# Eight loads of key and value weights move from SyncE's queue to GpSimd's in a trunk layer's prologue

## The chip, the cores and the metric

The kernel runs on one core of a Trainium2 chip. A core has five engines with an instruction stream each: TensorE (PE) multiplies matrices, VectorE (DVE), ScalarE (ACT) and GpSimd (POOL) work on rows of 128 partitions, SyncE (SP) only issues transfers (DMAs). The engines meet at semaphores. Transfers issued by any engine are carried out by the core's 16 DMA engines. The metric is the time of one execution on the device in microseconds. Before the change it is 1074.85 us, the median of three runs (1074.67 to 1075.89).

## The reference

One layer of a diffusion backbone runs over 128 context tokens and 512 latent tokens, 640 rows of width 1024, in float32. The part that the change touches is the start: a modulation is worked out from two conditioning vectors, applied to the normalised tokens, and the keys and values are columns 1024 to 1535 of the product with `w_in`.

```python
ada_ctx = (jax.nn.silu(c_ctx) @ w_ada[i] + b_ada[i])[None, None, :]
ada_lat = (jax.nn.silu(c) @ w_ada[i] + b_ada[i])[:, None, :]
...
def trunk_layer(h, ada, p, rope_tabs, ctx_k, ctx_v):
    sh1, sc1, g1, sh2, sc2, g2 = jnp.split(ada, N_ADA, axis=-1)
    u = rms_norm(h, p["g_pre1"]) * (1 + sc1) + sh1
    mo, k, v = mixer(u, p, rope_tabs, ctx_k, ctx_v)
    h = h + g1 * rms_norm(mo, p["g_post1"])
    u = rms_norm(h, p["g_pre2"]) * (1 + sc2) + sh2
    h = h + g2 * rms_norm(conv_ffn(u, p), p["g_post2"])
    return h, k, v
...
def mixer(u, p, rope_tabs, ctx_k, ctx_v):
    z = u @ p["w_in"]
    ...
    q, k, v, b_gate, c_gate, x_in, g_att, g_conv = jnp.split(z, idx, axis=-1)
```

Behind it follow attention over latent and cached context keys, a gated convolution, the output projection, and a feed-forward part with a convolution of width 3.

## The kernel before

All products are made in three passes: each float32 operand is split into a rounded part (`whi`, `UH`) and the rest (`wlo`, `UL`), and PE multiplies high by high, high by low and low by high (`mm3`, lines 234 to 237).

The prologue computes the keys and values. Its steps are these.

- The tokens: five tiles of 128 rows, `XT[:, t, :]`, 0.52 MB each, are loaded by SP (line 410). For each tile ACT sums the squares (`square`, line 435), POOL makes the variance and its root (`rstd_of`, lines 282 and 283), DVE scales the rows (`normal`, line 440), PE turns them (`x_turn`, line 447), and ACT or DVE copies them out (`x_copy`, lines 453 and 455).
- The modulation: scale and shift of the 1024 features are worked out in six groups of one or two blocks of 128 features, `GROUPS = ((0,), (1,), (2, 3), (4, 5), (6,), (7,))`. A group of one block takes two loads of 0.52 MB of `w_ada`, a group of two takes four (`ada_loads`, line 405). They go to tiles called `araw` and, for later groups, into the room of token tiles that are used up. PE multiplies them with the conditioning vectors (`ada1_mm`, line 478), ACT copies the result (line 486), PE adds up the pieces (lines 491 to 498), and DVE writes scale and shift, `scsh` (lines 503 and 505).
- `modulate` (lines 520 to 524) makes block f of the modulated tokens, `UH` and `UL`, on ACT and DVE.
- The key and value weights come in eight units, one for each block of 128 features: 128x512 floats, 0.26 MB. `fetch(i)` loads all units below i that aren't loaded yet. There are three buffers called `raw`, of two units each: units 0 and 1 share the first (raw_161 in the lists below), 2 and 3 the second, 4 and 5 the third, 6 and 7 the first again. `cut_upto` splits a unit on ACT and DVE (lines 592 and 594 for the first, 200 and 201 for the others).
- PE adds up keys and values over the eight blocks for the five token tiles (`kv_first`, line 531, for part of block 0, then `kv_mm`, by lines 235 to 237).

Units 8 and 9 of `units` are later weights of 4x256 columns, and go through `fetch` too.

What sets the order: PE, ACT, DVE and, in the prologue, SP run their instructions in the order in which the code is written. POOL's are put in order by the scheduler of the framework, which may move an instruction ahead when its buffers are free. A load into a buffer that is in use waits on its queue until the readers are done, and so do all behind it.

Of the kernel before, what the change touches and what calls it, by code (L numbers as in the profile page):

```python
# [22 lines left out]
KT = 8  # L23
# [89 lines left out]
def trunk_layer(ctx, tc, x_prompt, x_sample, cache_k, cache_v, c, c_ctx, w_ada, b_ada, g_pre1, g_post1, g_pre2,  # L113
                g_post2, w_in, q_norm, k_norm, w_att_out, conv_w, w_conv_out, w_o, w_up, conv_ffn, w_down, rope,
                y_prompt, y_sample, new_k, new_v):
    nc = tc.nc
    V, S, G, PE = nc.vector, nc.scalar, nc.gpsimd, nc.tensor
# [52 lines left out]
    def ps1():  # L170
        turn[1] += 1
        return psa.tile([128, 512], F32, tag=f"s1{turn[1] % 2}", name=nm("s1"), bufs=1)
# [7 lines left out]
    state = {"next": 0, "raw": [], "cut": [], "limit": 10}  # L180

    def raw_tile():
        return wp.tile([128, 1024], F32, tag="raw", name=nm("raw"), bufs=3)
# [22 lines left out]
    def fetch(i):  # L206
        while len(state["raw"]) < min(i, len(units), state["limit"]):
            w, k0, nk, c0, n = units[len(state["raw"])]
            if nk * n > 512:
                raw = raw_tile()  # L210
            else:

                if not halves:
                    raw = raw_tile()
                    halves.extend([raw[:, 512:1024], raw[:, 0:512]])
                raw = halves.pop()
            nc.sync.dma_start(raw[:, :nk * n].rearrange("p (k c) -> p k c", c=n),
                              w[k0 * 128:(k0 + nk) * 128, c0:c0 + n].rearrange("(k p) c -> p k c", p=128))
            state["raw"].append(raw)

# [6 lines left out]
    def next_unit():  # L227
        i = state["next"]
        state["next"] += 1
        fetch(i + 3)  # L230
        cut_upto(i + 2)
        return state["cut"][i]
# [141 lines left out]
    with tc.tile_pool(name="pro", bufs=2) as pro, tc.manual_schedule(engines={mybir.EngineType.SP}):  # L374
# [34 lines left out]
        for t in range(NT):  # L409
            nc.sync.dma_start(XT[:, t, :], xrows(t))  # L410
        ada_loads(0, [araw_tile() for _ in range(2)])
        fetch(1)
        ada_loads(1, [araw_tile() for _ in range(2)])
        fetch(2)

        def features():
# [174 lines left out]
        raw = state["raw"][0][:, 0:512]  # L591
# [41 lines left out]
        for f in range(2, KT):  # L633
# [42 lines left out]
            if f == KT - 2:  # L676
                cut_upto(9)
                p = ps1()
# [568 lines left out]
    def bank(i):  # L1247
        if i >= 2 and len(pools) == 1:
            early.close()
            pools.append(ctx.enter_context(tc.tile_pool(name="pb", bufs=1, space=bass.MemoryType.PSUM)))  # L1250
        return pools[i >= 2].tile([128, 512], F32, tag=f"b{i}", name=nm(f"b{i}"))
# [784 lines left out]
    for q in range(4):  # L2036
# [11 lines left out]
        elif q == 1:  # L2048
            half_load(0)
            p = bank(6)  # L2050
# [18 lines left out]
        for t in range(NT):  # L2069
# [5 lines left out]
            if q == 3 and t == 2:  # L2075
                p = bank(7)
# [448 lines left out]
```

## Time and profile before

| | |
|---|---|
| median of three runs | 1074.85 us |
| profiled execution | 1074.79 us, of it a span of 1073.0 us from the first to the last instruction |
| busy in the span: PE, DVE, ACT, POOL | 98%, 84%, 56%, 12% |
| chain of waits: share of PE | 90% |
| mean granted PE clock | 0.999 of full speed |
| moved from and to memory | 164.02 MB, a mean of 153 GB/s |

The profile gives times from the first instruction on. "L217" is line 217 of the kernel; "SPq" is SP's instruction that issues a transfer, and its length is the time that the issue took, not that of the transfer. A bracket at the end of a row is the time that the engine stood idle ahead of it and who released it. PEld is PE's loading of weights, which runs beside PE's multiplication.

### The profile page before, as it was taken

The page shows a single profiled execution, that of the slowest core. Times are in us where ns is not written, and L with a number is a line of the kernel's source. Part 1 is how long each engine was busy: PE and PEld are TensorE (multiplying, and loading weights), DVE is VectorE, ACT ScalarE, POOL GpSimd, SP SyncE. Part 2 cuts the span into 40 slices and gives each one's busy share as a digit, 9 for nine tenths or more (in the row PEclk, how much of TensorE's full clock was granted, in tenths as well). Part 3 has the DMA queues.
Part 4 walks back from the last instruction along what each step waited for, and adds up shares of the span by engine and source line. Part 5 has one row for each costly group of instructions (what it writes and reads, how often), then busy time and mean ns, then how long its engine had stood idle before and what let it go on. Part 6 is the DMA issues. An engine that isn't in the chain of part 4 may idle for free.

```text
span 1073.0 us, 20652 instructions
## 1 busy us (share of the span) xinstructions
PE 1056.8 (98%) x8216; PEld 995.4 (93%) x8216; DVE 899.9 (84%) x1379; ACT 598.4 (56%) x1057; POOL 133.1 (12%) x162
## 2 busy tenths in 40 slices
PE   8999999999999999999999999999999999999997
PEld 6788898899999999999998789999999999999996
DVE  5699999865498999896599678889999988989897
ACT  5478999942344544445322366645555555546673
POOL 1087676500000000000000020000000000000001
PEclk9999999999999999999999999999999999999999
DMA  9829999962244333223668634434544534436873
GB/s 320 256 82 175 190 168 187 191 147 60 75 123 124 93 103 94 79 79 99 189 188 253 198 131 129 121 116 136 166 131 152 150 122 131 152 116 219 277 275 115
DMA packets 243197, 164.02 MB, mean 153 GB/s; under 512 B 94874, under 2 KB 216214, under 8 KB 243102
## 3 DMA queue, kind: packets, MB, share of 16 engines
q1 hardware_dynamic: 242990, 162.68, 55.5%
q8 instruction: 64, 1.05, 0.4%
q14 instruction: 31, 0.25, 0.1%
q10 hardware_dynamic: 112, 0.04, 0.0%
HBM read 123.31 MB, written 17.36 MB: 131 GB/s over the span
## 4 chain that ended last, share of the span: by engine, by line
PE 90%; DVE 3%; ACT 2%; DMA 1%; POOL 1%; issue 1%; SPq 1%; DVEq 0%; ACTq 0%; POOLq 0%
PE b L1274 47%; PE b L235 10%; PE b L237 10%; PE b L236 9%; PE s L709 4%; PE s L1073 2%; PE s L1170 2%; PE s L235 1%; PE s L237 1%; PE s L1162 1%; PE s L478 1%; DVE marks L1120 1%; PE s L236 1%; PE b L1900 1%; ACT P L1134 1%
## 5 line engine op out<-in xcount | busy, mean ns | idle before, releaser
L1274 PE MATMUL b<-ZBr,whi 128*128 128x320 f32 x688 | 152.1, 309 | 0.0
L1274 PE MATMUL b<-MT,whi 128*128 128x320 f32 x608 | 134.4, 309 | 0.0
L1274 PEld LDWEIGHTS b<-ZBr,whi 128*128 128x128 f32 x688 | 114.9, 188 | 0.1
L1274 PE MATMUL b<-ZBr,wlo 128*128 128x320 f32 x344 | 106.1, 308 | 0.0
L1274 PEld LDWEIGHTS b<-MT,whi 128*128 128x128 f32 x608 | 101.7, 188 | 0.0
L1274 PE MATMUL b<-MT,wlo 128*128 128x320 f32 x304 | 94.0, 309 | 0.0
L1261 ACT ACTIVATE whi<-SUM 128x1024 fp32r<-128x1024 f32 x40 | 42.2, 1055 | 78.3 <-DVE SUM L1813 75.7
L1843 DVE SCALAR_TENSOR_TENSOR Y<-C,cffn,Y 128x642 f32<-128x642 f32 x88 | 77.9, 886 | 0.9
L1261 ACT ACTIVATE whi<-WB 128x1024 fp32r<-128x1024 f32 x38 | 40.2, 1058 | 55.5 <-DVE WB L1368 55.5
L1274 PE MATMUL b<-ZBT,whi 128*128 128x320 f32 x320 | 71.0, 308 | 0.0
L1274 PE MATMUL b<-UL,whi 128*128 128x320 f32 x228 | 70.8, 311 | 0.0
L1274 PE MATMUL b<-UH,wlo 128*128 128x320 f32 x228 | 70.1, 307 | 0.0
L1274 PE MATMUL b<-UH,whi 128*128 128x320 f32 x228 | 69.7, 306 | 0.0
L1282 ACT ACTIVATE p<-b 128x320 f32<-128x320 f32 x78 | 34.1, 437 | 55.3 <-PE b L1274 53.5
L1274 PEld LDWEIGHTS b<-ZBr,wlo 128*128 128x128 f32 x344 | 64.6, 188 | 0.0
L1265 DVE TENSOR_TENSOR wlo<-raw,whi 128x1024 fp32r<-128x1024 f32 (+1 forms) x51 | 50.4, 1020 | 13.4 <-ACT whi L1261 13.4
L1274 PEld LDWEIGHTS b<-MT,wlo 128*128 128x128 f32 x304 | 57.1, 188 | 0.0
L1274 PEld LDWEIGHTS b<-ZBT,whi 128*128 128x128 f32 x320 | 54.2, 188 | 1.6
L1120 DVE TENSOR_REDUCE marks<-s 128x1 f32<-128x640 f32 x64 | 52.1, 817 | 4.0 <-PE s L1073 3.8
L1265 DVE TENSOR_TENSOR wlo<-WB,whi 128x1024 fp32r<-128x1024 f32 x38 | 46.5, 1224 | 8.8 <-ACT whi L1261 8.7
L2355 POOL TENSOR_TENSOR ssqs<-ssqs 128x1 f32<-128x1 f32 x4 | 1.4, 356 | 412.9 <-ACT GJ L2349 412.9
L1261 ACT ACTIVATE whi<-raw 128x1024 fp32r<-128x1024 f32 (+1 forms) x51 | 43.5, 892 | 15.4 <-DMA raw<-in_w_o_dram 12.5
(477 smaller groups left out, 3348.1 us busy)
## 6 DMA issues: line engine op xcount, KB each, us to landing
raw<-in_w_in_dram SPq DMA_DIRECT2D x48, 512.0 KB
RAW<-in_w_up_dram SPq DMA_DIRECT2D x40, 512.0 KB
raw<-in_w_down_dram SPq DMA_DIRECT2D x22, 512.0 KB
GA<-in_w_ada_dram SPq DMA_DIRECT2D x16, 512.0 KB
actd<-Y SPq DMA_DIRECT2D x18, 321.0 KB
actl<-ACTb SPq DMA_DIRECT2D x18, 321.0 KB
A<-actl SPq DMA_DIRECT2D x9, 642.0 KB
A<-actd SPq DMA_DIRECT2D x9, 642.0 KB
```

The source lines that it names most:

```text
L235: PE.matmul(out, ah, bh, start=start, stop=False)
L236: PE.matmul(out, ah, bl, start=False, stop=False)
L237: PE.matmul(out, al, bh, start=False, stop=stop)
L709: PE.matmul(out, a, b, start=start and n == 0, stop=stop and n == 2, skip_group_check=True)
L1073: PE.matmul(o[h], q_of(hl, i, rows), kk[kx][rows, g, ks], start=m == 0, stop=m == 2, tile_position=(64 * h, 0), skip_group_check=True)
L1120: V.tensor_reduce(out=mk[:, h:h + 1], in_=s_of(), axis=AX.X, op=ALU.max, negate=True)
L1170: PE.matmul(p[64 * h:64 * h + 64, i * 128:i * 128 + 128], VH[:, w, s, vc_], src, start=k == 0 and m == 0, stop=k == ks[-1][0] and m == 2, ...
L1261: S.activation(to[0], raw, AF.Copy)
L1265: V.tensor_tensor(out=lo, in0=raw, in1=hi.bitcast(F32), op=ALU.subtract)
L1274: PE.matmul(out, p[:, ws], q[:, k, :], start=start and k == 0 and n == 0, stop=stop and k == 3 and n == 2, skip_group_check=True)
L1282: S.activation(t, pair[j][b], AF.Copy)
L1843: V.scalar_tensor_tensor(out=y, in0=crows(j)[i][:, d:d + NACT], scalar=cffn[:, 44 * d + o:44 * d + o + 1], in1=y, op0=ALU.mult, op1=ALU.add)
```

## The change

In `fetch`, the load is issued on `G`, GpSimd's queue, as long as fewer than KT = 8 units have been loaded, and on SP's queue from then on. The eight loads are those of the key and value units. All other loads keep their queue, and the modulation weights stay on SP.

```diff
@@ -214,7 +214,7 @@
                     raw = raw_tile()
                     halves.extend([raw[:, 512:1024], raw[:, 0:512]])
                 raw = halves.pop()
-            nc.sync.dma_start(raw[:, :nk * n].rearrange("p (k c) -> p k c", c=n),
+            (G if len(state["raw"]) < KT else nc.sync).dma_start(raw[:, :nk * n].rearrange("p (k c) -> p k c", c=n),
                               w[k0 * 128:(k0 + nk) * 128, c0:c0 + n].rearrange("(k p) c -> p k c", p=128))
             state["raw"].append(raw)
```

On POOL, at the start of the program, the scheduler puts the loads of units 0 to 5 right behind the setup (the identity matrix, ident), ahead of the variance var and root rstd of the first token tile. A row with a plus is new at its place, one with a minus has left it; "x2" stands for two loads, the halves of a buffer.

```order
 masks.py:199 AFFINE_SELECT ident<-ident 128x128
+L217 DMA raw_161<-in_w_in_dram 128x512 x2
+L217 DMA raw_256<-in_w_in_dram 128x512 x2
+L217 DMA raw_367<-in_w_in_dram 128x512 x2
 L282 TENSOR_SCALAR var_176<-ssq_174 128x1
+L282 TENSOR_SCALAR var_183<-ssq_181 128x1
 L283 TENSOR_TENSOR rstd_177<-var_176,mhalf 128x1
-L282 TENSOR_SCALAR var_183<-ssq_181 128x1
 L283 TENSOR_TENSOR rstd_184<-var_183,mhalf 128x1
```

Six loads came ahead of the first variance, and the second variance ahead of the first root. Further down, behind the root of the fifth token tile and ahead of the work that prepares the attention stage, stand units 6 and 7:

```order
 L283 TENSOR_TENSOR rstd_235<-var_234,mhalf 128x1
+L217 DMA raw_465<-in_w_in_dram 128x512 x2
 L765 MEMSET some 128x128
 L767 TENSOR_SCALAR backs<-ident 128x1 x2
```

They use the buffer of units 0 and 1 and wait there until both are split. On SP, the loads of the modulation weights (to araw and XT, line 405) follow one another from the tokens on, where units of raw stood between them:

```order
 L405 DMA araw_157<-in_w_ada_dram 128x8x128
 L405 DMA araw_158<-in_w_ada_dram 128x8x128
-L217 DMA raw_161<-in_w_in_dram 128x512
 L405 DMA araw_163<-in_w_ada_dram 128x8x128
 L405 DMA araw_164<-in_w_ada_dram 128x8x128
-L217 DMA raw_161<-in_w_in_dram 128x512
-L405 DMA XT<-in_w_ada_dram 128x4x256 x4
-L217 DMA raw_256<-in_w_in_dram 128x512 x2
-L405 DMA XT<-in_w_ada_dram 128x4x256
+L405 DMA XT<-in_w_ada_dram 128x4x256 x5
 L405 DMA araw_360<-in_w_ada_dram 128x4x256
```

No key or value load stands between them any more. The instructions of PE, DVE and ACT and their order are the same.

## The prediction

> **What bounds the kernel now.** I read the chain of waits first, because the change touches only the first 40 us and the question is what that stretch hangs on. Its rows are: start in us, length in us, what the chain goes through.
>
> ```profile
> 1.19 4.69 DMA XT<-in_x_sample_dram
> 5.90 0.45 SPq L405
> 6.39 4.00 SPq L217
> 10.44 6.48 DMA araw<-in_w_ada_dram
> 16.96 0.64 PE s L478 x16
> 17.61 2.45 PE s L531 x9
> ...
> 22.67 1.01 PE s L478 x32
> ...
> 25.28 1.38 PE s L478 x32
> ...
> 56.45 0.23 PE s L236
> ```
>
> Up to 16.96 us the chain is transfers and their issue; from there to 57 us it is nearly all TensorE (PE). So a load that lands later before 17 us moves PE's whole key/value stage, and one that lands later after that costs nothing until it eats its slack.
>
> Next the busy time by stretch: does the DMA have room? The last two columns are the DMA share and GB/s.
>
> ```profile
> core 0: us, PE busy (x) PEld busy (x) DVE busy (x) ACT busy (x) POOL busy (x), PEclk, DMA share, GB/s
> 3.00:9.00 6.00, 5.69 (x37) 5.26 (x35) 1.51 (x3) 3.24 (x5) 1.66 (x4) 1.00 0.99 380
> 9.00:17.00 8.00, 5.96 (x70) 4.62 (x72) 6.18 (x14) 5.26 (x14) 2.62 (x6) 1.00 1.16 310
> 17.00:25.00 8.00, 8.00 (x89) 5.63 (x89) 5.92 (x15) 4.48 (x10) 0.00 (x0) 1.00 1.07 351
> 25.00:30.00 5.00, 4.85 (x49) 3.38 (x47) 2.52 (x9) 2.34 (x6) 0.00 (x0) 1.00 1.11 353
> 65.00:70.00 5.00, 4.68 (x41) 4.71 (x41) 4.93 (x12) 2.89 (x7) 4.48 (x6) 1.00 0.00 0
> ```
>
> From 3 us to 30 us the DMA engines are full. PE works all of 17 to 25 us, at full clock. At 65 to 70 us nothing is loaded at all: what follows waits for work, not for transfers, so a late start is not caught up there.
>
> Last, the instructions that begin PE's stage, in order of time (start, length, engine, line, operation, wait before it in brackets).
>
> ```profile
> 4.67 1.06 ACT L435 ACTIVATE junk<-XT 128x1024 f32<-128x1024 f32 x1 [2.44 <-DMA XT<-in_x_prompt_dram]
> 5.90 0.19 POOL L282 TENSOR_SCALAR var<-ssq 128x1 f32<-128x1 f32 x1 [4.26 <-ACT junk L435]
> 6.76 0.75 DVE L440 TENSOR_SCALAR xn<-XT,rstd 128x1024 f32<-128x1024 f32 x1 [4.64 <-POOL rstd L283]
> ...
> 10.79 1.06 ACT L435 ACTIVATE junk<-XT 128x1024 f32<-128x1024 f32 x1 [0.19 <-DMA XT<-in_x_sample_dram]
> ...
> 13.96 1.28 DVE L455 COPY xTb<-s 128x512 f32<-128x512 f32 x2
> 14.45 1.07 PE L478 MATMUL s<-araw,s 128*32 128x128 f32 x28 [0.52 <-DMA araw<-in_w_ada_dram]
> ...
> 16.31 0.28 DVE L503 TENSOR_SCALAR scsh<-s,feat 128x2 f32<-128x2 f32 x1 [1.07 <-PE s L494]
> ...
> 16.96 0.64 PE L478 MATMUL s<-araw,s 128*32 128x128 f32 x16 [0.19 <-DMA araw<-in_w_ada_dram]
> 17.54 1.11 PE L531 MATMUL s<-whi,UH 128*128 128x512 f32 x3
> ```
>
> Two chains meet at the first key/value matmul (L531, 17.54). One is the modulation: PE starts the bulk of group 0 at 14.45, when its weights (araw) land, and scale and shift (scsh) come at 16.31. The other is the tokens: load, square on ACT, rstd on POOL, normalise on DVE, turn on PE, copy, the last copy for the first four token tiles ending at 15.24. The modulation came last; 16.31 − 15.24 = 1.1 us is the tokens' slack.
>
> **The change part by part.**
>
> SP loses eight issues, POOL gains eight. Six of them (units 0 to 5, three buffers that nobody holds yet) stand ahead of POOL's first variance; the last two wait for buffer raw_161 and stand behind the fifth rstd, with no POOL work queued behind them before the attention stage.
>
> *Bytes ahead of the modulation weights.* This is the main term. A load is 128x512 floats, 0.262 MB; six are 1.573 MB. Before, SP's order is tokens (2.62 MB), group 0 (1.05 MB), unit 0, group 1, unit 1. So group 0 has no key/value weight ahead of it, and group 1 has one. Now POOL can issue all six from the end of its setup on, while tokens and group 0 are still flowing. The engines are at 0.99 from 3 us, so what they move for POOL they do not move for SP. At 380 GB/s the six cost 1.573 / 0.380 = 4.1 us. How the two queues share matters little: tokens suffer first, group 0 the rest, and by the end of group 0 all six have been served if the shares are anywhere near even. Group 0 then lands at 14.45 + 4.1 = 18.6, and L531 starts at 17.54 + 4.1 = 21.6. Group 1 loses unit 0 from its front, so it is late by 5 × 0.262 / 0.380 = 3.4 us: 16.96 + 3.4 = 20.4, no longer last.
>
> Against this, the rate fell to 310 GB/s while SP's modulation weights flowed (9 to 17 us), so a second queue may use 70 GB/s that lay idle. Group 0 flows for about 1.05 / 0.310 = 3.4 us, so at most 0.24 MB or 0.6 us is covered; at least nothing. I take 0.3. Sum: 4.1 − 0.3 = **+3.8 us** at the first key/value matmul.
>
> The Trainium skill ("DMA: Bandwidth & Descriptors", Issuing engines are not separate DMA queues) says that transfers issued from different engines share the same 16 DMA engines, and that spreading them saves only issue time. By that the 4.1 us stands unreduced; the share of 0.99 at 3 to 9 us agrees, and no row of this kernel shows two busy queues together.
>
> *POOL's issues.* They are new on POOL, and the trace has no DMA issue of POOL. The nearest rows are SP's: a free queue and a full one.
>
> ```profile
> 0.74 0.39 SPq L410 DMA_DIRECT2D XT<-in_x_prompt_dram  x1
> ...
> 1.35 0.29 POOL masks.py:199 TENSOR_SCALAR_AFFINE_SELECT ident<-ident 128x128 f32<-128x128 f32 x1
> ...
> 12.84 2.19 SPq L217 DMA_DIRECT2D raw<-in_w_in_dram  x1
> ```
>
> POOL's setup ends at 1.64. Six issues at 0.39 free it at 4.0, before the first variance was due (5.90): no cost. Six at 2.19 free it at 14.8. I take 1.0, about the geometric mean of the ends and nearer the free queue, since POOL's own queue starts empty: free at 7.6, 1.7 us after the first variance was due. The order also puts the second variance ahead of the first rstd, 0.4 us more. The tokens are late anyway: sharing with POOL, they finish some 3 us later. Does that decide? DVE's row for this stretch, the length and then its busy time:
>
> ```profile
> 6.76:15.24 8.48, 7.04 (x13) 1.00 1.10 329
> ```
>
> It did 7.04 us of work in 8.48 us. With the modulation due at 16.31 + 4.1 = 20.4, the first normalise (6.76 before) may start as late as 20.4 − 7.04 = 13.4, so POOL may be free as late as 13.4 − 1.2 = 12.2, or (12.2 − 1.64) / 6 = 1.76 us an issue. Below that the issues cost nothing; at the upper end they decide (rival B).
>
> *SP without the eight issues.* SP spent 4.00 us in the issue of unit 0 with a full queue. Its modulation loads move up, but into an engine set that is full; no gain by itself.
>
> *After the start.* PE is on the chain, so its delay is carried whole, unless it now waits for loads. It doesn't: group 2 has 2 of the 6 loads already ahead of it before, so it is late by 4 × 0.262 / 0.380 = 2.8 us, less than PE's 3.8. Groups 3 to 5 follow in the same way: group 3 had four of the loads ahead of it, now eight at most, 2.8 us again. ACT's waits for unit 1 (0.74 us) and unit 2 (2.18) vanish:
>
> ```profile
> 15.73 0.62 ACT L592 ACTIVATE whi<-raw 128x512 fp32r<-128x512 f32 x1
> ...
> 19.60 0.63 ACT L200 ACTIVATE whi<-raw 128x512 fp32r<-128x512 f32 x1 [0.74 <-DMA raw<-in_w_in_dram]
> 20.69 0.38 ACT L486 ACTIVATE e<-s 128x256 f32<-128x256 f32 x1 [0.46 <-PE s L478]
> ...
> 26.24 0.63 ACT L200 ACTIVATE whi<-raw 128x512 fp32r<-128x512 f32 x1 [2.18 <-DMA raw<-in_w_in_dram]
> ```
>
> but the copy behind the first (L486) waited for PE, not for ACT, and PE waited for neither. No gain. Units 6 and 7 come earlier, from a free buffer; nobody waited for them.
>
> *The sum.* The profiled execution took 1074.79 us (span 1073.0), 0.06 below the median of 1074.85. 1074.79 + 3.8 = **1078.6 us**, +0.35%. A measurement of this kernel can tell 0.2% (2.15 us) from no change.
>
> **The rivals.**
>
> *B, POOL's issues become the bound.* At 2.19 us each POOL is free at 14.8, the first normalise starts at 16.0, DVE's 7.04 us end at 23.0 and scsh comes after that: 23.0 − 16.31 = +6.7, **1081.5 us**. For it: all token work hangs behind these six instructions, and the queue they feed meets full engines. Against it: POOL's queue starts empty, and its loads need not wait for SP's. The Trainium skill ("SBUF — State Buffer", Who interferes with whom) says that a VectorE operation in its two-port mode blocks GpSimd, which must write the descriptors of its own DMAs; that would stretch the issues. Before 6.76 us DVE ran only two reduces, so by that rule little is blocked unless the issues are slow already, and no run here shows it.
>
> *C, POOL's loads are served only in what SP leaves* (the other side). If they got no more than the idle 70 GB/s from 9 us on, unit 0 would be in at 9 + 0.262 / 0.070 = 12.7, plus the lag of 2.1 us between the end of group 0's bytes (9 + 3.4 = 12.4) and its use at 14.45: 14.8, still before its first use at 15.73; unit 1 some 3.7 us later, before 19.60. Group 0 would be no later than before, and group 1 earlier by 0.7; the tokens' copies still end at 15.24, so L531 could start at most 1 us sooner. **1074.8 us**, at best 1073.8: not slower. It decides as long as less than 2.15 × 0.380 = 0.82 MB of the six loads get ahead of group 0. Against it: nothing in the trace ranks one queue below another.
>
> **How the numbers follow.** The sum as worked out 0.64, B 0.17, C and whatever lies between C and the bound 0.14; 0.05 stays for a gain over 2.15 us, for which I find no place. Slower: 0.64 + 0.17 = 0.81; same 0.14; faster 0.05. The likeliest case alone spans 1077.5 (0.6 us covered, some lag less) to 1079.5. The range reaches from the middle of C's stretch, 1075.8, to a little past B, 1082.0.
>
> **What would show it.** Right: SP's first two groups of modulation loads have no key/value load between them; 375 to 390 GB/s still at 3 to 9 us, with a second queue of about 2 MB; the last token square near 13 to 14 us (10.79 before); group 0's matmuls near 18.3; L531 near 21.3; PE from there to the end of the stage as long as before (39 us); no ACT wait for raw. Wrong: POOL issues longer than 1.76 us and the first normalise after 13.4 us (B); group 0's matmuls still near 14.5 (C); or PE waiting again after 22 us for modulation loads, which would add to the 3.8.

## The result and the profile after

The changed kernel took 1079.27 us, the median of five runs (1079.06 to 1079.86), beside 1075.55 us, the median of five runs of the kernel before: a ratio of 1.0034 with a 95% interval of 1.0023 to 1.0045. It is slower by 0.34%. In a second series of runs, shown below, the same changed kernel came to 1.0047 (1.0035 to 1.0059).

The chain of waits after, the same columns as before:

```profile
1.19 4.82 DMA XT<-in_x_sample_dram
6.02 11.64 DMA araw<-in_w_ada_dram
17.70 1.92 PE s L478 x28
19.62 1.05 PE s L447 x4
20.89 0.95 PE s L447 x4
21.85 1.01 PE s L478 x16
22.86 2.56 PE s L531 x9
...
30.63 1.01 PE s L478 x32
```

The chain still begins with the tokens and group 0 of the modulation weights. But group 0's 28 matmuls begin at 17.70 instead of 14.45, and take 1.92 us. Before, they took 1.07. The busy time by stretch shows why (the column after POOL is the granted PE clock, then the DMA share and GB/s):

```profile
3.00:9.00 6.00, 4.65 (x28) 4.41 (x27) 0.75 (x1) 2.66 (x5) 3.84 (x8) 1.00 1.01 392
9.00:17.00 8.00, 4.61 (x37) 3.68 (x37) 5.60 (x11) 4.69 (x11) 2.21 (x6) 0.97 1.11 345
17.00:25.00 8.00, 7.30 (x62) 5.68 (x63) 4.73 (x12) 3.38 (x7) 0.00 (x0) 0.60 1.14 325
25.00:30.00 5.00, 5.00 (x64) 3.50 (x63) 2.34 (x8) 2.55 (x6) 1.16 (x2) 1.00 1.11 352
```

From 17 to 25 us PE was granted 0.60 of full speed, where it had 1.00 before. The instructions at the beginning of PE's stage, and the new ones on POOL:

```profile
1.61 3.47 POOL L217 DMA_DIRECT2D raw<-in_w_in_dram  x6
6.03 0.19 POOL L282 TENSOR_SCALAR var<-ssq 128x1 f32<-128x1 f32 x1 [0.95 <-ACT junk L435]
...
13.59 1.06 ACT L435 ACTIVATE junk<-XT 128x1024 f32<-128x1024 f32 x1 [1.19 <-DMA XT<-in_x_sample_dram]
...
17.70 1.92 PE L478 MATMUL s<-araw,s 128*32 128x128 f32 x28 [1.31 <-DMA araw<-in_w_ada_dram]
...
22.79 1.23 PE L531 MATMUL s<-whi,UH 128*128 128x512 f32 x3
```

Six issues took POOL 3.47 us, 0.58 each, and it was free 0.95 us before the first variance. The last token tile came 2.8 us later than before (13.59 against 10.79), group 0 3.25 us later, and the first key/value matmul (L531) 5.25 us later. The difference, 2.0 us, was lost between 17.70 and 22.79. I put it down to the lower clock, and the experiments test that.

### The profile page after: what moved, and what is told of

It reads as the page before. It is cut to its first block, busy times and chain, and to the rows that moved or that the text cites. A ratio compares the mean times of both kernels' runs of the same rounds, so it can differ in the third digit from the quotient of the medians.

```text
span 1077.3 us, 20660 instructions
## 1 busy us (share of the span) xinstructions
PE 1058.5 (98%) x8216; PEld 997.3 (93%) x8216; DVE 899.7 (84%) x1379; ACT 598.1 (56%) x1057; POOL 137.3 (13%) x170
## 3 DMA queue, kind: packets, MB, share of 16 engines
q8 instruction: 64, 1.05, 0.4%
## 4 chain that ended last, share of the span: by engine, by line
PE 91%; DVE 3%; ACT 2%; DMA 2%; POOL 1%; issue 1%; DVEq 0%; SPq 0%; ACTq 0%; POOLq 0%
PE b L1274 47%; PE b L235 10%; PE b L237 10%; PE b L236 9%; PE s L709 4%; PE s L1073 2%; PE s L1170 2%; DMA araw<-in_w_ada_dram 1%; PE s L478 1%; PE s L1162 1%; PE s L235 1%; PE s L237 1%; PE s L236 1%; PE b L1900 1%; DVE marks L1120 1%
```

## The experiments

My theory after the result had two parts. First, the loads on POOL's queue take bandwidth ahead of group 0, and that alone makes it late; the queue itself costs nothing. Second, PE stands idle so much while it waits that its clock is halved, and this adds 2 us. The main rival was that POOL's queue costs by itself, by its issues or its way of making transfers.

**The same order without POOL.** The edit is against the kernel before.

```diff
+        fetch(6)
         ada_loads(0, [araw_tile() for _ in range(2)])
         fetch(1)
```

> Units 0 to 5 stay on SyncE's queue but are issued there between the tokens and group 0 of the modulation weights; nothing goes to GpSimd. Theory (bytes ahead of group 0, plus a colder TensorE clock while it waits): group 0's 28 matmuls start at 14.45 + 4.1 = 18.5 us, no earlier than in the changed kernel (17.7), the granted clock falls to 0.5 for some us, and the time is 1079 to 1081 us. Rival (the loss comes from GpSimd's queue, its issues or its descriptors): group 0 is late only by what the order costs less than that, and the time is clearly below the changed kernel, 1075 to 1077 us.

It took 1080.13 us, a ratio of 1.0044 (1.0031 to 1.0056). Its PE row (added lines shift the numbers a little: L479, and L480 or L476 further down, are L478 of the two kernels):

```profile
18.77 1.92 PE L479 MATMUL s<-araw,s 128*32 128x128 f32 x28 [1.08 <-DMA araw<-in_w_ada_dram]
```

Group 0 came 4.3 us later than before, and the clock in 17 to 25 us was 0.57. The whole loss is there with nothing on POOL. So the order of the bytes is enough to explain it, with the clock's part in it.

**The lower clock taken away.** Three transposes of the identity are added ahead of token tile 2, eight ahead of tile 3 and twelve ahead of group 0. They write parts of tiles that are overwritten or not read. The edit is against the changed kernel.

```diff
             p = xps[t]
+            for _ in range({2: 3, 3: 8}.get(t, 0)):
+                PE.transpose(p[:, 0:128], ident, ident)
...
-        ada1_mm(0, 0)
+        pas[0] = ps1()
+        for _ in range(12):
+            PE.transpose(pas[0][:, 384:512], ident, ident)
         ada1_mm(0, 1)
```

> The changed kernel with 23 extra transposes of the identity in TensorE's gaps before group 0 (3 ahead of token tile 2, 8 ahead of tile 3, 12 ahead of group 0), whose results are overwritten or not read. Theory: the granted clock stays at 1.00 from 17 to 25 us; group 0's matmuls still start near 17.7, its 28 take 1.1 instead of 1.9 us, the first key/value matmul comes at 17.7 + 3.1 = 20.8 instead of 22.8, and the time falls by 2.0 us to about 1077.3. Rival (the lower clock lies beside other work and costs nothing): the clock stays up and the time stays at 1079.3.

It took 1077.87 us, 1.0026 (1.0016 to 1.0037). The clock stayed at 1.00 and the 28 matmuls took 1.07 us again, but in this profile group 0 began at 18.75, 1.05 us later than in the changed kernel's, so the first key/value matmul was only 1.2 us earlier (21.61). To compare fairly, the changed kernel and this one ran again, side by side.

> The changed kernel again, beside the next kernel on the same chip. Theory: group 0's matmuls between 17.5 and 18.8 us, the clock at 0.5 for 6 to 8 us, 1079.3 us.

> The changed kernel with the 23 extra transposes, again: in the first run the clock stayed up as expected, but group 0's weights happened to land 1.05 us later in its profile than in the changed kernel's, and the gain was 1.2 us at the first key/value matmul. Theory: with the same landing the gap from group 0's matmuls to the first key/value matmul is 2.9 us instead of 5.1, and the time is 1.4 to 2.2 us below the changed kernel beside it. Rival (the clock costs nothing in the end): the two times agree within 0.4 us.

The changed kernel took 1080.03 us, 1.0047 (1.0035 to 1.0059); with the extra transposes it took 1077.65 us, 1.0026 (1.0016 to 1.0037): 2.4 us less, a little above the expected 1.4 to 2.2, and every run of the one lies above every run of the other. With the clock up, 2.7 us of loss remain in both series (1077.65 against 1074.99 for the kernel before, 1077.87 against 1075.20): that is what the order of the bytes costs. The two rows of the kernel with the transposes, and then those of the changed kernel, whose profile here is that of its slowest run (1081.69 us, with the clock at half for 10.2 us, longer than the expected 6 to 8):

```profile
17.49 1.07 PE L480 MATMUL s<-araw,s 128*32 128x128 f32 x28 [0.94 <-DMA araw<-in_w_ada_dram]
...
20.35 1.33 PE L533 MATMUL s<-whi,UH 128*128 128x512 f32 x3
```

```profile
18.80 1.92 PE L478 MATMUL s<-araw,s 128*32 128x128 f32 x28 [1.07 <-DMA araw<-in_w_ada_dram]
...
23.88 1.07 PE L531 MATMUL s<-whi,UH 128*128 128x512 f32 x3
```

From group 0 to the first key/value matmul it is 2.86 us with the clock up and 5.08 us with it down. That difference of 2.2 us doesn't depend on when group 0 landed. The landing itself moved by 1.1 us between two profiles of the changed kernel (17.70 and 18.80), so single profiles of it can differ by as much.

The control is the kernel before with the same transposes.

> The kernel before with the same 23 extra transposes. Theory: its clock was at 1.00 already, so they bring nothing: first key/value matmul at 17.5 to 18.0, within 0.5 us of the kernel before in time (1074.9 to 1075.9). Rival (the extra transposes help for another reason): 1.4 us or more faster here too.

It took 1074.73 us, 0.9996 (0.9988 to 1.0005): they bring nothing where the clock was up already. Its first key/value matmul came at 17.43, just below the expected range.

**Fewer units early.** The first units alone go to POOL, the others stay on SP. The lines are compared with those of the changed kernel.

```diff
-            (G if len(state["raw"]) < KT else nc.sync).dma_start(...
+            (G if len(state["raw"]) < 2 else nc.sync).dma_start(...
```

> Only units 0 and 1 go to GpSimd's queue, early; units 2 to 7 stay on SyncE's as before the change. Theory (cost by bytes ahead of group 0): 0.524 MB at 380 GB/s, so group 0's matmuls start at 14.45 + 1.4 less some mixing, 15.5 to 15.9 us; the time is 1075.5 to 1076.5 us, or up to 1077.5 if the clock falls here too. Rival (the cost is that of using GpSimd's queue at all): nearly the full loss, 1078 to 1079.5 us.

It took 1075.85 us, 1.0004 (0.9996 to 1.0013). Group 0 came at 15.16, 0.7 us late, a little less than the expected range, and in the profiled run the clock stayed up. The same edit with 4 in place of 2:

> Units 0 to 3 go early to GpSimd's queue, 4 to 7 stay on SyncE's. Theory (cost by bytes): 1.049 MB ahead of group 0, 2.75 us at 380 GB/s, and by the two-unit run (0.7 us for 0.524 MB) and the changed kernel (3.25 us for 1.573 MB) between 1.4 and 2.2: group 0's matmuls start at 15.9 to 16.7 us. With the clock up, 1076.2 to 1077 us; if it falls, up to 1078.5. Rival (a fixed cost from the second buffer on): like the changed kernel, 17.5 us and 1079 us.

It took 1078.01 us, 1.0025 (1.0014 to 1.0035). The first row is that of two units, the second that of four:

```profile
15.16 1.07 PE L478 MATMUL s<-araw,s 128*32 128x128 f32 x28 [0.49 <-DMA araw<-in_w_ada_dram]
```

```profile
16.97 1.92 PE L478 MATMUL s<-araw,s 128*32 128x128 f32 x28 [1.29 <-DMA araw<-in_w_ada_dram]
```

Four units make group 0 2.5 us late, above the range that I gave and near the plain 2.75 us by bytes. At four the clock falls too (1.92 us for the same matmuls). So the loss grows with the bytes and takes a step with the clock, between two and four units. Since the landing of one kernel moves by 1.1 us, 2.5 us for four units against 3.0 to 4.4 for six don't by themselves rule out a fixed price from the second buffer on; the one-queue run, which has the whole loss without POOL, speaks against a price of the queue.

**The queue, but later.** All eight loads are on POOL, behind the five roots, with idle memsets to hold them apart. POOL's instructions follow the code in this one, and the calls `fetch(1)` and `fetch(2)` at their old places are taken out.

```diff
         square(4)
+        hold = pro.tile([128, 1024], F32, name="hold", bufs=1)
+        for n in (2, 4, 6):
+            fetch(n)
+            for _ in range(4 if n < 6 else 0):
+                G.memset(hold, 0.0)
```

> All eight loads on GpSimd's queue as in the change, but behind the five token roots (about 13 us) and in three stages with four idle memsets of 128x1024 between them (units 0 and 1, then 2 and 3, then 4 and 5, then 6 and 7 when their buffer is free). Theory: group 0's matmuls start at 14.4 to 14.8 us as before the change, the clock stays at 1.00, the first key/value matmul is at 17.5 to 18.3, and the time is 1074.5 to 1076 us. Rival (the queue costs, not the moment): 1078 to 1080 us.

It took 1078.9 us, 1.0035 (1.0024 to 1.0046): the total is the rival's. The rows point to another reason.

```profile
13.22 1.79 POOL L217 DMA_DIRECT2D raw<-in_w_in_dram  x2
```

```profile
14.62 1.07 PE L476 MATMUL s<-araw,s 128*32 128x128 f32 x28 [0.48 <-DMA araw<-in_w_ada_dram]
...
19.94 1.82 PE L529 MATMUL s<-whi,UH 128*128 128x512 f32 x3 [2.42 <-ACT UH L518]
```

```profile
18.87 0.63 ACT L595 ACTIVATE whi<-raw 128x512 fp32r<-128x512 f32 x1 [2.86 <-DMA raw<-in_w_in_dram]
```

Group 0 was on time, as the theory had it (14.62). Now unit 0 was late: issued from 13.22 on, it was ready at 18.87, where its split could have begun at 16.0 (18.87 less the wait of 2.86). A load of 0.26 MB into full engines took 5.6 us from the start of its issue. My expectation had left that out. PE waited 2.4 us and its clock fell again (0.79 in 17 to 25 us).

So units 0 and 1 went back to their places on SP, and units 2 to 7 to POOL with four memsets ahead of units 2 and 3, and four more ahead of 4 and 5, again with POOL's instructions in the order of the code. The first two lines are compared with those of the changed kernel.

```diff
-            (G if len(state["raw"]) < KT else nc.sync).dma_start(...
+            (G if 1 < len(state["raw"]) < KT else nc.sync).dma_start(...
...
+        for n in (4, 6):
+            for _ in range(4):
+                G.memset(hold, 0.0)
+            fetch(n)
```

> Units 0 and 1 on SyncE's queue in their old places; units 2 to 7 on GpSimd's queue, held back to about the old moments: behind the five roots and four idle memsets (about 17 us) units 2 and 3, four memsets later (about 22 us) 4 and 5, then 6 and 7 when their buffer is free. Theory (what is late is what lies behind other bytes; the queue itself costs nothing): group 0's matmuls at 14.4 to 14.8 us, the first key/value matmul at 17.4 to 17.9, the clock 1.00 throughout, and 1074.5 to 1075.8 us. Rival (GpSimd's queue costs by itself, by slower loads or by what it does to SyncE's): 1077 us or more.

It took 1077.36 us, 1.0024 (1.0012 to 1.0036), again within the rival's range; its eleven runs spread from 1076.19 to 1082.53. The first key/value matmul was at 17.52, as expected, and then:

```profile
24.96 1.07 PE L478 MATMUL s<-XT,s 128*32 128x128 f32 x30 [1.82 <-DMA XT<-in_w_ada_dram]
```

```profile
17.25 1.33 POOL L217 DMA_DIRECT2D raw<-in_w_in_dram  x2
```

Units 2 and 3, issued at 17.25 while group 2's modulation weights were on the way, made those late. Before, on one queue, they stood behind four loads of group 2. The clock fell to 0.66 in 25 to 30 us. The last step holds them back further (eight memsets, then six).

> As the run with units 2 to 7 held back on GpSimd's queue, but held longer: units 2 and 3 eight idle memsets behind the fifth root (about 21 us), 4 and 5 six memsets after that (about 28 us). There, issued at 17.3 us, units 2 and 3 overtook group 2's modulation weights, which SyncE had issued by 20.4, and TensorE waited 1.8 us for them at 23 us. Theory (a load on the second queue goes ahead of what waits on the first; the queue costs nothing else): issued at 21 us they no longer overtake group 2, first key/value matmul at 17.4 to 17.9 us, no wait of TensorE above 0.5 us after it, the clock 1.00 throughout, and 1074.5 to 1075.7 us. Rival (GpSimd's queue costs by itself): again 1077 us or more.

It took 1076.25 us, 1.0009 (1.0001 to 1.0018): 0.5 us above the range that I gave, and below the rival's. In this profile the first key/value matmul came at 16.52, a microsecond earlier than expected, so the loss arose behind it. It has a row, with a wait of PE above the 0.5 us that I had allowed:

```profile
27.30 0.63 ACT L200 ACTIVATE whi<-raw 128x512 fp32r<-128x512 f32 x1 [3.39 <-DMA raw<-in_w_in_dram]
```

```profile
28.14 0.61 PE L498 MATMUL s<-sel,e 128*128 128x4 f32 x4 [0.69 <-ACT e L486]
```

Group 2 was no longer made late and the clock stayed at 1.00. Unit 2, issued from 21.09, was ready at 27.30, and the copy behind its split kept PE waiting for 0.69 us. Six of the eight loads are on POOL here, and the loss is 0.09% (at most 0.18% by its interval), with a place in it for a late load. A cost of the queue itself for these six is at most that.

No version beat the kernel before: the nearest are the control (0.9996) and the two units (1.0004), and neither can be told from it.

## Why the prediction was right, and where a step failed

The forecast of 1078.6 us (+0.35%) lies 0.7 us under the measured 1079.27, and what was measured is the mechanism of the likeliest case: bytes ahead of the modulation weights. That the size came out so well is in part luck, since two errors went in opposite directions. The bytes alone cost 2.7 us of time, as the runs with the clock up show, and not 3.8; and the clock, for which the sum had no term, added 1.0 to 2.4 us (the whole loss was 3.7 us in the first series and 5.0 in the second).

- *Bytes ahead of group 0*, +3.8 us at group 0's matmuls, 18.25. Measured 17.70 in the first profile of the changed kernel and 18.80 in the second; with the extra transposes 18.75 and 17.49. The mean of the four is 18.2. Right in size, with a spread that I hadn't foreseen. The 0.3 us within it, for an idle share that a second queue could use, was read wrongly: the rate of 310 GB/s in 9 to 17 us stood beside a DMA share of 1.16, so the engines weren't idle, only slower. It rose to 345 GB/s in the changed kernel, but to 346 in the one-queue order too, so no second queue is needed for it. I put it down to the longer rows of the key weights, which no run tried apart.
- *The step that failed*: "L531 starts at 17.54 + 4.1", which carried over the 3.09 us between group 0 and the first key/value matmul as they stood before. It measured 5.09 us, since the clock fell (from 1.00 to 0.50 at about 16.6 us). The sum had no term for PE's clock, and the first stretch quoted ahead of it showed a PE at full clock without asking what held it there. The runs with extra transposes, where that gap was 2.86 us, put the term at 2.0 us against the gap before and 2.2 against their own.
- *Carried whole*: nearly. The delay was 5.25 us at 22.79 and 4.95 us at group 3's matmuls (38.33 against 33.38). The second of group 2's two pieces in the chain shrank from 1.38 to 1.01 us because its weights no longer kept PE waiting (at 25.28 before, at 30.63 after). The prediction had counted no such gain.
- *The spans* differ by 4.3 us, though at the last score matmuls of the attention the delay is still 4.9 (220.3 against 215.4). The missing 0.6 us was not won by the changed kernel; this profile of the kernel before lost it. There, the last transposing transfer of the attention (rows below) stands in the chain of waits, ahead of PE, and in the first profile of the changed kernel it doesn't. In the kernel before with the extra transposes, the same stretch began at the same time (the last score matmuls at 215.5 in both) and ended 0.7 us earlier (the last matmuls of L1170 at 225.5 against 226.2). In the second profile of the changed kernel that transfer is in the chain as well (L1145 at 226.21), so this varies between runs.

```profile
219.52 2.35 SPq L1145
221.97 3.35 DMA PT<-P
225.36 1.03 PE s L1170 x30
```

- *POOL's issues*: 0.58 us each, nearer the lower end than the 1.0 taken, and hidden, as the break-even of 1.76 us said. Rival B didn't happen.
- *Rival C* (loads served only in what SP leaves) didn't happen: the tokens were 2.8 us late.
- *What would show it*: the last token square at 13.59 (13 to 14 forecast), 2.10 MB on a second queue, no ACT wait for raw, and a stage as long as before (39.1 us from L531 to the end of the keys and values at 61.89, 39.4 before) were right. The rate at 3 to 9 us was 392 GB/s, just above the 375 to 390 forecast. L531 near 21.3 was wrong (22.79).

## What to carry to other kernels

A second queue is no second set of transfer engines: at 3 to 9 us they moved 380 GB/s before and 392 after. Where they are full, moving loads to another queue lets them take bandwidth from loads that stood ahead of them, so write down what lies ahead of the load that the chain hangs on, before and after. When PE is made to wait longer at the beginning of a stage, look at its busy share in the few microseconds before it starts, and price the same matmuls at half clock if that share falls to about a half or below. And a load issued on the second queue just when it is needed comes late when the engines are full: here it was ready 5.6 and 6.2 us after its issue began.

## What the runs showed of the hardware that I had not expected

The clock fell without PE being idle all the time. The stretch 13 to 17 us, PE's busy time and then its clock, in the kernel before, the changed one, with two units and with four, in this order:

```profile
13.00:17.00 4.00, 3.29 (x52) 1.00 1.18 301
```

```profile
13.00:17.00 4.00, 1.48 (x12) 0.95 1.19 297
```

```profile
13.00:17.00 4.00, 3.25 (x48) 1.00 1.20 290
```

```profile
13.00:17.00 4.00, 1.51 (x16) 0.86 1.21 290
```

At 3.25 us of 4 it stayed, at 1.5 us of 4 it fell to half and stayed there, in the changed kernel, from 16.57 until 23.40 us, 5.7 us after PE was at work again.

Cut finely, the traces show how such a fall goes. The clock was at half for 3.41 us in the first two runs with held-back loads (20.44 to 23.85 and 26.31 to 29.72), for 6.83 us in the changed kernel, the one-queue order and the run with four units, and for 10.24 us in the second profile of the changed kernel (13.91 to 24.15): one, two or three steps of 3.41 us. In the step ahead of each of the six falls PE was busy for 0.07 to 1.62 us. The clock also falls at the end of each profile, where the work runs out, so the steps can be counted through all twelve. There, every step at full clock in which PE worked for 1.62 us or less is followed by half clock, and none with 1.72 us or more is. The clock came back after steps with at least 3.31 us of work, and not after steps with 2.18 to 2.34 us at half clock. So in these traces the clock looks to be set once in each step of 3.41 us, and to fall when PE was busy for less than about half of the step. The steps lie differently in each run, so the fixed stretch of 13 to 17 us is only a rough measure. With two units it was close: the step from 10.53 to 13.95 had 1.78 us of work, and the mean clock of its eleven runs lies between 0.996 and 0.999, so in some of those without a profile it may have fallen.

The Trainium skill ("TensorE: Matmul & The Clock Gate", Part 1: The HAM clock gate) says that the clock is halved after an idle window of about 3.4 us. The traces agree with the half clock and with the time, but PE was at work for up to 1.62 us of such a window, so an idle window is to be read as one with little work.

How the transfer engines share between two queues stays open. Of two loads issued on POOL from 21.09 us, beside a full queue of SP, the first was ready at 27.30. That is 0.26 MB in 6.2 us, 42 GB/s, or 84 if both came together: an eighth to a quarter of the 349 GB/s of that stretch. But six loads issued at the start made group 0 3.0 to 4.4 us late, where their bytes take 4.1 us at 380 GB/s. Which share holds when wasn't measured.
